# Mixer loads at other places: weight tiles, next values, p fetches, token sums and decay tables of a hybrid encoder layer

## The chip, the cores and the metric

The kernel runs on one core of one Trainium2 chip. The metric is the device time of one execution in microseconds (us); lower is better. The core has five engines with queues of their own: TensorE (PE, matrix products; its weight loads are shown as PEld), VectorE (DVE), ScalarE (ACT), GpSimd (POOL) and SyncE (SP), which here does nothing but issue DMA transfers. Each engine runs its instructions in order, and one that waits holds up all behind it.

## The reference

One post-norm layer of an encoder, in fp32, for x of 1024 tokens by 1024 features:

```
u    = x @ w_in                                   # split into rq, rk, rv, rg, aq, ak, av
yR   = swish(rg) * GroupNorm(retention fwd + bwd) # 8 heads of 64, chunks of 128, decays from ret_decay
yA   = windowed attention, +-128 tokens, 8 q heads on 2 kv heads, ALiBi, a sink logit per head
h    = LN1(alpha * x + concat(yR, yA) @ w_out)
f    = (silu(h @ w_gate) * (h @ w_up)) @ w_down + sigmoid(h @ w_ple_gate) * (p @ w_ple_proj)
out  = LN2(alpha * h + f)
```

`p` is 1024 tokens by 256. The decays of retention are log1p(-2^ret_decay), one per head and direction.

## The kernel before, in words

**Arithmetic.** An fp32 product is made of three matmuls of a faster type: each operand is cut into a high part (an ACT copy, recorded at L51) and a low part (a DVE subtraction, L107), by `split`, and `mm3` (L110 to L112) multiplies high by high, high by low and low by high. So every operand that PE uses passes through ACT and DVE first.

**Stages.** First the input projections of the parts that the mixers need at once, in units `punits` of a Strassen-like scheme (seven products for each pair of weight tiles, `Proj`); after unit 8 the loop calls `tables()`, which makes the decay tables: a power on POOL (L196), then a chain of small operations on DVE and two on ACT with table loads. Then the mixers, four pairs of heads i = 0 to 3, each with `Retention` (values rv, keys rk, queries rq, decay mask dt) and `Attention` (scores, sc, transposed by trn, multiplied by val). Then the output projection with LN1, the per-layer gate with p (`ple`), the feed-forward products, and LN2. After the mixers everything is one schedule written by hand; it includes the token sums of `ple`.

**The mixers.** The order of PE, POOL and SP is the order of the program text there. DVE and ACT are ordered by a scheduler, which by and large follows when operands come. Operations wrapped in `in_order` are chained on ACT and DVE to stay behind each other. A script (L836 to L848) lists the steps of a pair; each `F` in it takes the next few steps from a queue. This queue, built by `enqueue`, holds the rest of the projections as ten tiles of 16 steps: AQI[2], RKI[3], RQI[3], embedding(0), AQI[3], embedding(1) and four gates. A step of a projection is three matmuls of 128x512 (one `mm3`); the last of eight copies a bank to a tile `es` and stores it in DRAM (`ud`, L746; a gate multiplies it in place instead). While one tile's steps run, the next tile's raw weights are loaded and cut, attached to steps 0, 6, 9 and 12 of the tile before.

**Embedding.** `embedding(h)` multiplies p by one half of w_ple_proj. For each of 8 blocks t of tokens a fetch (L767) brings pT[t] to a tile `pr` (two buffers), `prep` cuts it to `p` (two buffers), two steps multiply, and the result goes through `es` to `ed` by SP (L797). At the first step of block t the kernel fetches t+2 and cuts t+1.

**Raw buffers.** Raw weights, q's raw tile (`load_pair`, L546) and rv's raw tile (`rv_load`, L537) share one ring `raw` of two buffers: a new load waits until the tile two before it is read. `load_pair(i+1)` loads rk, rq and q of the next pair (`more[0]` in the script), `rv_load(i+1)` its values (`more[1]`), `cq[g]` converts q, `nt[h]` transposes rv (PE, L523), to be copied by ACT.

**Token sums.** In `ple`, `to_T(t)` (L1009 on) builds for a block t of tokens the sums x1, x2 and x3 that the seven products need, and at once cuts x2 into TT[2] and stores a copy of h (`keep_h`). Side work is handed to `prod` in four slots per product.

Of the kernel before, what the change touches and what calls it, by code (L numbers as in the profile page):

```python
# [20 lines left out]
NT = S // P  # L21
# [19 lines left out]
def layer(tc, xT, xn, w_first, w_mt, w_out, w_pg, w_pe, pT, w_gu, w_dn,  # L41
# [21 lines left out]
    def in_order(f):  # L63

        def g(*args):
            behind_act[1] = True
            f(*args)
            behind_act[1] = False

        return g  # L70
# [107 lines left out]
    lt = cp.tile([P, 4, 24], F32, name="lt")  # L178
# [14 lines left out]
    def tables():  # L193
        t_, u_, d_, m_ = (lt[:, i, :] for i in range(4))
        pool.tensor_copy(masks, mraw)
        pool.tensor_tensor(t_, cst[:, C_TWO:C_TWO + 1].to_broadcast([P, 24]), rr, ALU.pow)  # L196
        dve.tensor_scalar(u_, t_, -1.0, 1.0, ALU.mult, ALU.add)
        act.activation(rr, u_, AF.Ln)
        dve.tensor_scalar(d_, u_, 1.0, None, ALU.subtract)
        dve.tensor_scalar(m_, d_, 0.0, None, ALU.is_equal)  # L200
        dve.tensor_tensor(d_, d_, m_, ALU.subtract)
        dve.tensor_tensor(rr, rr, m_, ALU.subtract)
        dve.reciprocal(m_, d_)
        dve.tensor_tensor(rr, rr, m_, ALU.mult)
        dve.scalar_tensor_tensor(lg, rr, -1.0, t_, ALU.mult, ALU.mult)
        act.activation(kd[:, 0, :], lg[:, 0:8], AF.Exp, scale=cst[:, C_KF:C_KF + 1])
        act.activation(kd[:, 1, :], lg[:, 8:16], AF.Exp, scale=cst[:, C_KB:C_KB + 1])
        dve.tensor_scalar(kd, kd, 0.125, None, ALU.mult)
        act.activation(cd, lg[:, 16:24], AF.Exp, scale=float(P))
        dve.tensor_scalar(skb, skb, -1.0, None, ALU.mult)  # L210
# [167 lines left out]
    with tc.manual_schedule(engines={ET.PE, ET.DVE, ET.Activation, ET.Pool, ET.SP}):  # L378
        zero = tt([P, HF], "s1", 2, mybir.dt.bfloat16)
        pool.memset(zero, 0.0)  # L380
        zb = bank("o")
        for _ in range(WARM):
            pe.matmul(zb, zero[:, :P], zero, start=True, stop=True)
        for (m, h), t in zip([(m, h) for m in range(4) for h in range(2)], [t for t in ("mm", "s", "t", "o") for _ in range(NB[t])]):
            st[m, h] = bank(t)
        for kt in range(KT):
            r = A[kt]
            if kt % 2 == 0:
                xp = big16()
            xt = xp[:, :, kt % 2, :]  # L390
            if kt == 0:
                w0 = rawt(2 * HF)
                sp.dma_start(w0[:, :HF], w_first[0][:, :HF])
                for h in range(2):
                    sp.dma_start(r[:, hs[h]], xT[kt][:, hs[h]])
                sp.dma_start(w0[:, HF:], w_first[0][:, HF:])

                def first_w(j):
                    wt_ = wp.tile([P, 2, HF], F32R, tag="w", bufs=4, name=nm("w"))
                    wr = w0[:, j * HF:(j + 1) * HF]  # L400
                    dve.tensor_copy(wt_[:, 0, :], wr)
                    dve.tensor_tensor(wt_[:, 1, :], wr, wt_[:, 0, :].bitcast(F32), ALU.subtract)
                    return wt_

                wf = [first_w(0)]
            else:
                if kt % 2 == 0:
                    wr = rawt(2 * HF)
                    sp.dma_start(wr, w_first[kt // 2])
                sp.dma_start(r, xT[kt])  # L410
                if kt % 2 == 0:
                    wf = []
                    for i in range(2):
                        t = wp.tile([P, 2, HF], F32R, tag="w", bufs=4, name=nm("w"))
                        split(wr[:, hs[i]], t[:, 0, :], t[:, 1, :])
                        wf.append(t)
            if kt == 1:
                wf.append(first_w(1))
            w = wf[kt % 2]
            for h in range(2):  # L420
                split(r[:, hs[h]], xt[:, 0, hs[h]], xt[:, 1, hs[h]])
            xs.append(xt)
            for m, h in ([(m, h) for m in range(4) for h in range(2)] if kt else [(m, h) for h in range(2) for m in range(4)]):
                mm3(st[m, h], w[:, 0, m * P:(m + 1) * P], w[:, 1, m * P:(m + 1) * P],
                    xt[:, 0, hs[h]], xt[:, 1, hs[h]], kt == 0, kt == KT - 1)
            if kt > 4:
                x_put(kt - 5)
            if kt >= 4:
                x_sums(kt - 4)
        for n in range(2):  # L430
            projs[n].load()
        consts_in()
        pahead(2)
        first = [atile() for _ in range(4)]
        for m in range(4):
            t = first[m]
            act.activation(t[:, hs[0]], st[m, 0], AF.Copy)
            dve.tensor_copy(t[:, hs[1]], st[m, 1])
        pahead(4)
        x_put(3)  # L440
        for k, (pr, p) in enumerate(punits):
            pr.mm(p)
            pr.post(p, k)
            if pr is projs[-1]:
                {6: lambda: keys(hs[0]), 5: lambda: keys(hs[1]), 7: lambda: queries(hs[0]),
                 2: lambda: queries(hs[1])}.get(p, lambda: None)()
            pahead(k + 1 + min(5, 4 + k))
            while late and late[0][0] <= k:
                late.pop(0)[1]()
            if k == 8:  # L450
                tables()
        for _, f in late:
            f()

# [47 lines left out]
    def enqueue(tiles):  # L502

        def both(f, g):
            f()
            g()

        for f in tiles[0][0]:
            f()
        for n, (_, steps) in enumerate(tiles):  # L510
            if n + 1 < len(tiles):
                for k, f in zip((0, 6, 9, 12), tiles[n + 1][0]):
                    steps[k] = lambda f=f if k == 0 else in_order(f), g=steps[k]: both(f, g)
            queue.extend(steps)


# [239 lines left out]
    def embedding(h):  # L756

        hold = {}

        wpe, ps = [], {}  # L760

        prs = {}

        def fetch(t):
            if t < NT:
                prs[t] = bt([P, 2 * P], "pr", 2)
                sp.dma_start(prs[t], pT[t])  # L767

        def prep(t):
            if t < NT:  # L770
                ps[t] = bt([P, 2, 2 * P], "p", 2, F32R)
                split(prs[t], ps[t][:, 0, :], ps[t][:, 1, :])

        raw = {}

        def load():
            raw["r"] = rawt(2 * HF)
            sp.dma_start(raw["r"], w_pe[h])
            fetch(0)
            fetch(1)  # L780

        def cut(q):
            wpe.append(atile((P, 2, HF), F32R))
            split(raw["r"][:, hs[q]], wpe[q][:, 0, :], wpe[q][:, 1, :])

        def step(t, q):
            if q == 0:
                fetch(t + 2)
                in_order(prep)(t + 1)
                hold["b"] = bank("mm")  # L790
            b, pt = hold["b"], ps[t]
            c = slice(q * P, (q + 1) * P)
            mm3(b, pt[:, 0, c], pt[:, 1, c], wpe[q][:, 0, :], wpe[q][:, 1, :], q == 0, q == 1)
            if q:
                e = bt([P, HF], "es", 2)
                act.activation(e, b, AF.Copy)
                sp.dma_start(ed[t][:, hs[h]], e)  # L797

        return [load, lambda: cut(0), lambda: cut(1), lambda: prep(0)], [lambda t=t, q=q: step(t, q) for t in range(NT) for q in range(2)]

    def run(steps, total):

# [10 lines left out]
    F = None  # L813
    with tc.manual_schedule(engines={ET.PE, ET.Pool, ET.SP}):
        enqueue([spill(AQI[2]), spill(RKI[3]), spill(RQI[3]), embedding(0), spill(AQI[3]), embedding(1)] + [gate(i) for i in range(4)])
        turn_rv = rv_load(0)
        for i in range(NPAIR):
# [4 lines left out]
            sco, trn, val = (lambda n: (a.scores, n)), (lambda n: (a.turn, n)), (lambda n: (a.values, n))  # L822
# [11 lines left out]
            else:  # L834
# [1 line left out]
            run(first_steps + [  # L836
                C(1), K(2), sco(1), F, C(2), K(3), F, trn(0), sco(2), ws[1], F, C(3), (r.scan,), val(0), F, trn(1), sco(3), F,
                val(1), Y(0, 0), ws[2], F, trn(2), sco(4), F, val(2), Y(0, 1), N(0), F, trn(3), sco(5), M(0), ws[3], F,
                val(3), Q(1), more[0], F, trn(4), sco(6), F, val(4), Y(1, 0), ws[4], F, trn(5), sco(7), more[1], cq[0], F,
                val(5), Y(1, 1), N(1), ws[5], F, trn(6), cq[1], F, nt[0], nt[1], val(6), M(1), F, trn(7), ws[6], F], 36)  # L840
            val_last = val(7)
        run([val_last, F, X(0), F, X(1), F, F], 16)

# [172 lines left out]
    def to_T(t):  # L1016
# [12 lines left out]
        dve.tensor_tensor(x2, b1, x1, ALU.subtract)  # L1029
        dve.scalar_tensor_tensor(HB[1, 1][:, 1, :, cols(t)], b1, -1.0, h.bitcast(F32), ALU.mult, ALU.subtract)  # L1030
        dve.tensor_tensor(x3, x3, b1, ALU.subtract)
        put(2, x2, t)
        keep_h(t, act)

    def t3(t):
# [57 lines left out]
    def ple(ahead):  # L1093
# [21 lines left out]
        def c00(k):  # L1115
            act.activation(g[k], b1[k], AF.Sigmoid)
            if k % 2:
# [4 lines left out]
        s1 = quad()  # L1122
        to_T(4)
        prod(1, b1, True, False, lambda k: act.activation(s1[k], b1[k], AF.Copy),
             [L(to_T, 5), L(t4s, 4), L(to_T, 6), L(t4s, 5)])
        g = quad()
        prod(2, b1, False, True, c00, [L(to_T, 7), [], L(t4s, 6), L(t4s, 7)])
        by = banks(TO)
        u2 = quad()
        prod(6, by, True, False, plus(u2, s1, by), [L(t3, 4), L(t3, 5), L(t3, 6), L(t3, 7)])  # L1130
# [540 lines left out]
```

## Time and profile before

| what | value |
|---|---|
| time, median of 3 runs | 1221.87 us (1220.24 to 1222.24) |
| time of the profiled execution | 1221.87 us |
| its span on the core | 1219.7 us |
| mean granted TensorE clock | 0.995 |
| DMA | 186.81 MB in 72848 packets, 153 GB/s over the span |
| loads `raw<-in_w_mt` | 14 of 512 KB, median 3.7 us to landing |

How to read it: the span runs from the first to the last instruction that the profiler recorded. A row of the timeline gives start, duration, engine, line, operation, the tile written and the tiles read, the shape, and in brackets how long the engine stood idle before it and who released it; equal rows in a line are merged (x4), and their duration is then that of all. "SPq" rows are DMA issues, and a landing is the time from the issue until the data are there. A row of waits gives the total, the number and the longest. Line numbers are those of the kernel before; in the changed kernel the same lines stand 3 to 6 further down inside the first stage and the mixers (L537 becomes L543, L546 becomes L552, L767 becomes L773).

### The profile page before, as it was taken

The numbers are of one execution on the slowest core, as the hardware profiler recorded it, in microseconds if no ns is written. First come the engines' busy times: TensorE is split into PE (matmuls) and PEld (weight loads), VectorE is DVE, ScalarE is ACT, GpSimd is POOL, SyncE is SP. The second block draws the span as 40 slices with busy tenths as digits, with TensorE's granted clock in tenths as the row PEclk, the third lists the DMA queues.
The fourth block names the chain that finished last, engine by engine and source line by source line (L and its number), as shares of the span: only waits on it lengthen the run. The fifth ranks groups of instructions, "written<-read, shape, count | busy, mean of one in ns | idle before, by whom it ended". The sixth has DMA issues, their size and how long they took to land.

```text
span 1219.7 us, 16421 instructions
## 1 busy us (share of the span) xinstructions
PE 1195.1 (98%) x5911; PEld 985.5 (81%) x5911; DVE 764.3 (63%) x1258; ACT 525.3 (43%) x968; POOL 448.5 (37%) x379
## 2 busy tenths in 40 slices
PE   9999999989799999999999999999999999999997
PEld 7878888768688788878888888888888888888886
DVE  6964666657565538776555555555545556875677
ACT  4532456666766512473433332333223334653441
POOL 1651213130201002332455655666556523024235
PEclk9999999999999999999999999999999999999999
DMA  6222255572310333445244344543544149999977
GB/s 224 92 87 104 83 177 153 159 224 95 114 35 22 123 114 106 143 176 181 104 164 122 103 155 165 181 128 97 155 165 146 70 144 288 386 277 211 273 172 207
DMA packets 72848, 186.81 MB, mean 153 GB/s; under 512 B 8384, under 2 KB 10560, under 8 KB 72768
## 3 DMA queue, kind: packets, MB, share of 16 engines
q1 hardware_dynamic: 57344, 148.03, 34.4%
q0 software_dynamic: 13696, 31.46, 13.6%
q10 hardware_dynamic: 1728, 6.29, 1.3%
q8 instruction: 46, 0.75, 0.2%
q14 instruction: 34, 0.28, 0.1%
HBM read 128.87 MB, written 51.64 MB: 148 GB/s over the span
## 4 chain that ended last, share of the span: by engine, by line
PE 90%; DVE 5%; DMA 2%; POOL 1%; issue 1%; ACT 1%; DVEq 0%; SPq 0%; POOLq 0%; ACTq 0%
PE bs L318 5%; PE bs L320 5%; PE bs L319 5%; PE bmm L320 5%; PE bmm L318 5%; PE bmm L319 5%; PE bt L318 5%; PE bt L320 5%; PE bt L319 5%; PE bo L320 5%; PE bo L318 5%; PE bo L319 5%; PE bmm L110 4%; PE bmm L112 4%; PE bmm L111 4%; PE bo L731 2%
## 5 line engine op out<-in xcount | busy, mean ns | idle before, releaser
L107 DVE TENSOR_TENSOR w<-H,w 128x512 fp32r<-128x512 f32 x44 | 43.6, 991 | 67.3 <-ACT w L51 67.3
L51 ACT ACTIVATE sc<-sc,st 128x385 f32<-128x385 f32 (+3 forms) x128 | 71.3, 582 | 27.0 <-DVE st L701 17.8
L1167 POOL TENSOR_TENSOR H<-ln 128x512 f32<-128x512 f32 x22 | 33.0, 1500 | 126.0 <-DMA ln<-in_w_gu 126.0
L107 DVE TENSOR_TENSOR w<-raw,w 128x512 fp32r<-128x512 f32 x56 | 44.3, 798 | 47.5 <-ACT w L51 47.3
L1199 POOL TENSOR_TENSOR ev<-ev 128x512 f32<-128x512 f32 x33 | 52.1, 1579 | 56.5 <-DMA h<-in_w_dn 24.1
L107 DVE TENSOR_TENSOR u<-H,u 128x512 fp32r<-128x512 f32 x47 | 45.4, 967 | 40.3 <-ACT u L51 40.2
L1203 POOL TENSOR_TENSOR ev<-ev,ev 128x512 f32<-128x512 f32 x44 | 67.3, 1539 | 2.6
L51 ACT ACTIVATE ev<-ev 128x512 f32<-128x512 f32 x33 | 20.9, 632 | 107.0 <-DVE ev L1214 107.0
L110 PE MATMUL bmm<-H,w 128*128 128x512 f32 x144 | 61.4, 426 | 0.2 <-ACT H L51 0.2
L696 POOL COPY sc<-skb 128x2 f32<-128x2 f32 x32 | 6.0, 191 | 140.6 <-PE bt L716 114.4
L112 PE MATMUL bmm<-H,w 128*128 128x512 f32 x144 | 57.2, 397 | 0.0
L111 PE MATMUL bmm<-H,w 128*128 128x512 f32 x144 | 57.1, 396 | 0.0
L51 ACT ACTIVATE w<-raw 128x512 fp32r<-128x512 f32 x72 | 43.6, 622 | 25.9 <-PE bo L112 6.2
L893 POOL TENSOR_TENSOR stt<-stt,cst 128x1 f32<-128x1 f32 x8 | 11.5, 1451 | 99.4 <-DVE stt L892 99.4
L51 ACT ACTIVATE u<-H 128x512 fp32r<-128x512 f32 x47 | 29.5, 628 | 38.9 <-POOL H L1169 8.8
L51 ACT ACTIVATE u<-raw 128x512 fp32r<-128x512 f32 x43 | 26.2, 629 | 29.6 <-PE bt L320 8.0
L51 ACT ACTIVATE w<-H 128x512 fp32r<-128x512 f32 x44 | 27.4, 622 | 23.3 <-PE bmm L320 6.6
L701 DVE CUSTOM_DVE_ANT_0 sc<-cst,bs,skb 128x384 f32<-128x384 f32 (+1 forms) x64 | 35.1, 575 | 2.5 <-PE bs L700 2.2
L1171 POOL TENSOR_TENSOR H<-ln,raw 128x512 f32<-128x512 f32 x22 | 34.3, 1562 | 0.0
L110 PEld LDWEIGHTS bmm<-H,w 128*128 128x128 f32 x144 | 27.6, 192 | 6.7 <-issue 1.5
L1169 POOL TENSOR_TENSOR H<-H,raw 128x512 f32<-128x512 f32 x22 | 32.1, 1461 | 1.7
L1314 POOL DMA_DIRECT2D h<-in_w_dn x24 | 21.3, 899 | 31.2 <-issue 16.6
(857 smaller groups left out, 3994.1 us busy)
## 6 DMA issues: line engine op xcount, KB each, us to landing
ad<-ev SPq DMA_DIRECT2D x33, 512.0 KB, 2.9
raw<-in_w_gu SPq DMA_DIRECT2D x22, 512.0 KB, 5.5
ln<-in_w_gu SPq DMA_DIRECT2D x22, 512.0 KB, 4.3
raw<-ad SPq DMA_DIRECT2D x40, 256.0 KB, 5.8
ln<-ad SPq DMA_DIRECT2D x37, 256.0 KB, 6.5
H<-in_w_dn SPq DMA_DIRECT2D x33, 256.0 KB, 8.0
raw<-in_w_mt SPq DMA_DIRECT2D x14, 512.0 KB, 3.7
A<-in_w_pg POOLq DMA_DIRECT2D x12, 512.0 KB, 5.5
```

The source lines that it names most:

```text
L51: ins = nc.scalar.activation(*args, **kw)
L107: dve.tensor_tensor(lo, raw, hi.bitcast(F32), ALU.subtract)
L110: pe.matmul(o, lh, rh, start=start, stop=False)
L111: pe.matmul(o, lh, rl, start=False, stop=False)
L112: pe.matmul(o, ll, rh, start=False, stop=stop)
L318: pe.matmul(o, lh, rh, start=start, stop=False, skip_group_check=True)
L319: pe.matmul(o, lh, rl, start=False, stop=False, skip_group_check=True)
L320: pe.matmul(o, ll, rh, start=False, stop=stop, skip_group_check=True)
L701: dve.tensor_tensor_reduce(sc[:, g, :nk], cst[:, tc0:tc0 + nk], b[:, :nk], -slope(i, g), skb[:, 2 * i + g:2 * i + g + 1], ALU.add, ALU.min ...
L1171: pool.tensor_tensor(s[2], a(1, 0), a(0, 0), ALU.subtract)
L1199: pool.tensor_tensor(c[:, 1, :], c[:, 0, :], c[:, 1, :], ALU.mult)
L1203: pool.tensor_tensor(self.ev[dst][:, 0, :], left, right, op)
```

## The change

Five edits, all of order; the number of instructions on each engine stays the same, and so does PE's order.

1. `tables()` keeps its two POOL operations after unit 8; its DVE and ACT operations become `tables2()`, after unit 16.
2. `enqueue` attaches the next tile's load and cuts to steps 8, 12 and 14 (for the third tile 2, 6 and 8); for an embedding, which now has five functions, to 6, 10, 12, 13 and 14.
3. `embedding` starts with begin(0) and begin(1), each of which cuts a block and fetches the one two further; at the end of block t, behind the store, it cuts t+2 and fetches t+4.
4. In the script, `more[1]` (rv's load) stands behind sco(6) instead of sco(7), and `cq[0]` behind Y(1, 1).
5. `to_T` loses its last two lines to a new `t2(t)`, which side slots of the first two products call later.

```diff
@@ tables
         pool.tensor_tensor(t_, cst[:, C_TWO:C_TWO + 1].to_broadcast([P, 24]), rr, ALU.pow)
+
+    def tables2():
+        t_, u_, d_, m_ = (lt[:, i, :] for i in range(4))
         dve.tensor_scalar(u_, t_, -1.0, 1.0, ALU.mult, ALU.add)
...
             if k == 8:
                 tables()
+            if k == 16:
+                tables2()
@@ enqueue
-                for k, f in zip((0, 6, 9, 12), tiles[n + 1][0]):
-                    steps[k] = lambda f=f if k == 0 else in_order(f), g=steps[k]: both(f, g)
+                fs = tiles[n + 1][0]
+                for j, (k, f) in enumerate(zip((6, 10, 12, 13, 14) if len(fs) > 3 else (2, 6, 8) if n == 1 else (8, 12, 14), fs)):
+                    steps[k] = lambda f=in_order(f) if j else f, g=steps[k]: both(f, g)
@@ embedding
             if q == 0:
-                fetch(t + 2)
-                in_order(prep)(t + 1)
                 hold["b"] = bank("mm")
...
                 sp.dma_start(ed[t][:, hs[h]], e)
+                in_order(prep)(t + 2)
+                fetch(t + 4)
+
+        def begin(t):
+            prep(t)
+            fetch(t + 2)
+
-        return [load, lambda: cut(0), lambda: cut(1), lambda: prep(0)], ...
+        return [load, lambda: cut(0), lambda: cut(1), lambda: begin(0), lambda: begin(1)], ...
@@ script of a pair
-                val(3), Q(1), more[0], F, trn(4), sco(6), F, val(4), Y(1, 0), ws[4], F, trn(5), sco(7), more[1], cq[0], F,
-                val(5), Y(1, 1), N(1), ws[5], F, trn(6), cq[1], F, nt[0], nt[1], val(6), M(1), F, trn(7), ws[6], F], 36)
+                val(3), Q(1), more[0], F, trn(4), sco(6), more[1], F, val(4), Y(1, 0), ws[4], F, trn(5), sco(7), F,
+                val(5), Y(1, 1), cq[0], N(1), ws[5], F, trn(6), cq[1], F, nt[0], nt[1], val(6), M(1), F, trn(7), ws[6], F], 36)
@@ to_T, ple
-        put(2, x2, t)
+
+    def t2(t):
+        put(2, X[t][1], t)
         keep_h(t, act)
...
-             [L(to_T, 5), L(t4s, 4), L(to_T, 6), L(t4s, 5)])
+             [L(to_T, 5) + L(t2, 4), L(t2, 5) + L(t4s, 4), L(to_T, 6), L(t2, 6) + L(t4s, 5)])
-        prod(2, b1, False, True, c00, [L(to_T, 7), [], L(t4s, 6), L(t4s, 7)])
+        prod(2, b1, False, True, c00, [L(to_T, 7), L(t2, 7), L(t4s, 6), L(t4s, 7)])
```

What this does to the order of an engine's rows is seen at three places. The first is SP in pair 2, from the end of embedding(1) to the load of rv for pair 3. `raw` is the ring of two, `rkq` holds rk and rq, `ed` and `es` are the embedding's stores; L141 loads the first gate's weight tile. Before:

```order
L797 DMA ed<-es_2919 128x512
L543 DMA rkq_2952<-ud 128x1024
L544 DMA rkq_2953<-ud 128x1024
L546 DMA raw_2956<-ud 128x1024
L797 DMA ed<-es_2963 128x512
L797 DMA ed<-es_3000 128x512
L141 DMA raw_3003<-in_w_mt 128x1024
L537 DMA raw_3058<-ud 128x1024
```

And after:

```order
L773 DMA pr_2810<-in_pT 128x256
L141 DMA raw_2840<-in_w_mt 128x1024
L801 DMA ed<-es_2849 128x512
L801 DMA ed<-es_2913 128x512
L549 DMA rkq_2949<-ud 128x1024
L550 DMA rkq_2950<-ud 128x1024
L552 DMA raw_2953<-ud 128x1024
L801 DMA ed<-es_2960 128x512
L543 DMA raw_2997<-ud 128x1024
L801 DMA ed<-es_3003 128x512
```

The weight tile has moved from behind q's raw tile to ahead of it. The load of rv therefore takes the buffer of the weight tile, no longer that of q's raw tile.

The second place is SP at the start of embedding(0); `pr` are the fetches of p, and L746 (L752) stores a projection's bank. Before:

```order
L778 DMA raw_1786<-in_w_pe 128x1024
L767 DMA pr_1788<-in_pT 128x256
L767 DMA pr_1790<-in_pT 128x256
L746 DMA ud<-es_1917 128x512
L746 DMA ud<-es_2040 128x512
L141 DMA raw_2070<-in_w_mt 128x1024
L767 DMA pr_2072<-in_pT 128x256
L797 DMA ed<-es_2084 128x512
L767 DMA pr_2104<-in_pT 128x256
```

And after:

```order
L784 DMA raw_1877<-in_w_pe 128x1024
L773 DMA pr_1879<-in_pT 128x256
L773 DMA pr_1881<-in_pT 128x256
L752 DMA ud<-es_1914 128x512
L773 DMA pr_2008<-in_pT 128x256
L773 DMA pr_2039<-in_pT 128x256
L752 DMA ud<-es_2047 128x512
L801 DMA ed<-es_2084 128x512
L773 DMA pr_2090<-in_pT 128x256
```

Blocks 2 and 3 are now fetched before the first step of the embedding, and the next tile's weight load (L141) is gone from among the fetches; it stands behind the last of them.

The third place is ACT at the first step of embedding(1), in pair 2. `sc` are attention scores, `p<-pr` the high parts of p, and the first `es` of each piece the copy of the last bank of the tile before the embedding, AQI[3]. Before:

```order
L51 ACTIVATE p_2598<-pr_2420 128x256
L51 ACTIVATE sc_2616,st_2579<-sc_2616,st_2579 128x385 x2
L51 ACTIVATE es_2652<-bmm_2549 128x512
L51 ACTIVATE sc_2616<-sc_2616,st_2579 128x384 x2
L51 ACTIVATE p_2659<-pr_2422 128x256
L51 ACTIVATE ptr_2674<-bt_2671 128x256
```

And after:

```order
L51 ACTIVATE sc_2613,st_2576<-sc_2613,st_2576 128x385 x2
L51 ACTIVATE es_2659<-bmm_2546 128x512
L51 ACTIVATE sc_2613<-sc_2613,st_2576 128x384 x2
L51 ACTIVATE p_2628<-pr_2484 128x256
L51 ACTIVATE p_2636<-pr_2486 128x256
L51 ACTIVATE ptr_2674<-bt_2671 128x256
```

The cut of block 0 has moved from ahead of that `es` to behind it and behind the two `sc` copies, next to the cut of block 1.

More of the change, by code (lines that the diff above doesn't have):

```diff
@@ L797, in step @@
                 sp.dma_start(ed[t][:, hs[h]], e)
-        return [load, lambda: cut(0), lambda: cut(1), lambda: prep(0)], [lambda t=t, q=q: step(t, q) for t in range(NT) for q in range(2)]
+                in_order(prep)(t + 2)
[3 more added lines that the diff above has]
+            fetch(t + 2)
+        return [load, lambda: cut(0), lambda: cut(1), lambda: begin(0), lambda: begin(1)], [lambda t=t, q=q: step(t, q) for t in range(NT) for q in range(2)]
     def run(steps, total):
```

## The prediction

> **What bounds the kernel now.** I read the page first, then TensorE's waits, then the timeline around each wait of the mixers, the decay tables and the token sums. Busy time and the chain of waits on the page, then who TensorE (PE) waited for (total us, times, longest):
>
> ```profile
> PE 1195.1 (98%) x5911; PEld 985.5 (81%) x5911; DVE 764.3 (63%) x1258; ACT 525.3 (43%) x968; POOL 448.5 (37%) x379
> ```
>
> ```profile
> engine line waited for: us in total, times, longest us
> PE bt L523 <- DMA raw<-ud: 6.0, 1, 6.0
> PE bmm L110 <- ACT p L51: 5.6, 6, 3.3
> PE bs L699 <- DVE pt L617: 0.8, 2, 0.6
> PE bt L318 <- DVE A L1113: 0.7, 1, 0.7
> PE bs L318 <- DVE A L297: 0.6, 1, 0.6
> PE bmm L112 <- DVE p L107: 0.6, 2, 0.4
> ```
>
> PE is the bound, and the change alters neither its instructions nor their order. So the change can only move PE's gaps. The rows name five it aims at: the transposition of rv (L523), the `p` splits (two rows), the token sums (L1113), the tables (L297). The row of L699 is one it may lengthen. The profiled execution took 1221.87 us, 2.17 more than its span of 1219.7; that is also the median of the three runs shown, so sums go against 1221.87. About 0.2% (2.4 us) is what a measurement of this kernel tells from no change.
>
> A wait costs PE a little more than its idle time. PE's timeline around the longest wait for `p` (start, duration):
>
> ```profile
> 254.01 0.40 PE L112 MATMUL bmm<-A,p 128*128 128x512 f32 x1
> 257.73 0.50 PE L110 MATMUL bmm<-A,p 128*128 128x512 f32 x1 [3.32 <-ACT p L51]
> 258.06 0.40 PE L111 MATMUL bmm<-A,p 128*128 128x512 f32 x1
> 258.30 0.39 PE L112 MATMUL bmm<-A,p 128*128 128x512 f32 x1
> 258.53 0.82 PE L716 MATMUL bt<-cst,sc 128*128 128x128 f32 x6
> ```
>
> Back to back these matmuls start 0.23 apart (258.30 to 258.53). Across the wait it is 3.72, so 3.49 is lost where 3.32 is listed: 0.17 more per wait.
>
> **Gains, part by part.** *The p waits.* ACT's timeline, and from the chain in order of time the two transfers of `pr` that end in long waits; then the landing of all 16:
>
> ```profile
> 257.26 0.42 ACT L51 ACTIVATE p<-pr 128x256 fp32r<-128x256 f32 x1 [3.50 <-DMA pr<-in_pT]
> ```
>
> ```profile
> 227.38 6.83 DMA pr<-in_pT
> 250.03 7.21 DMA pr<-in_pT
> ```
>
> ```profile
> DMA to landing us min/median/max: 1.9/3.3/7.2
> ```
>
> A fetch goes out two weight-tile steps ahead of its split, and what is late is the transfer that takes about 7 us, beside the 512 KB loads of the same queue; ACT, which runs in order, stands for it with an es copy behind. The change gives the fetch four steps and puts the loads behind the last fetches. With the median landing of 3.3 all eight waits go: 5.6 + 0.6 + 8 x 0.17 = 7.6. (With 7.2 some stay: a rival below.)
>
> *rv(3).* What SP's L537 waited for, its issue, the landing of its three transfers, and PE with its clock in stretches around it (length, PE busy, granted clock, DMA share):
>
> ```profile
> SPq L537 <- DVE q L354: 13.2, 1, 13.2
> ```
>
> ```profile
> 329.72 0.32 SPq L537 DMA_DIRECT2D raw<-ud x1
> ```
>
> ```profile
> DMA to landing us min/median/max: 3.1/3.5/3.7
> ```
>
> ```profile
> 226.20:263.10 36.90, 31.12 (x230) 1.00 0.73 226
> 266.59:269.86 3.27, 3.27 (x27) 1.00 0.33 94
> 332.95:338.51 5.56, 5.56 (x26) 0.56 0.42 106
> ```
>
> ```profile
> 326.80:331.00 4.20, 0.19 (x1) 1.00 0.06 17
> 331.00:338.00 7.00, 5.05 (x24) 0.51 0.47 145
> ```
>
> The load wanted the raw buffer that the q conversions of pair 3 held. In the changed order the first gate's weight tile is loaded ahead of load_pair(3), so of the two buffers rv(3) takes that tile's, free at its second cut, which stands some eight weight-tile steps before the transposition. A step takes about 1.9 (31.1 busy for 16, in the row of 226.20 above), so the load has some 15 us for its 3.5. The wait goes, 6.0 + 0.17 = 6.1. So does the slow clock behind it: 4.2 us into the idle stretch the granted clock falls to 0.51, and the matmuls from L523 to the next L716 took 5.56 against 3.27 a pair earlier: 2.3.
> The Trainium skill (TensorE: Matmul & The Clock Gate, What's actually happening) says the same of the cause, half the pulses after an idle window of about 3.4 us and full clock after as long a busy one; by it the debt would be 3.4 us at half speed, so 1.7 us in place of 2.3, and the forecast 0.6 higher. Here the clock came back 6.8 us after it fell, 5.05 of them busy.
>
> *Tables and token sums.* POOL's pow, for which DVE's and ACT's table operations stood in order, with PE's A (L297) behind them, and DVE's half of the u splits, ahead of L1113:
>
> ```profile
> 73.95 4.62 POOL L196 TENSOR_TENSOR lt<-cst,rr 128x24 f32<-128x24 f32 x1
> ```
>
> ```profile
> 536.40 2.50 DVE L948 TENSOR_TENSOR u<-raw,u 128x512 fp32r<-128x512 f32 x4 [3.38 <-ACT u L51]
> ```
>
> The pow now has eight units of products to end in, and the short operations behind it start at once. The wait of 0.6 + 0.17 goes, though DVE still has them to do: 0.2 is left as a loss (0 to 0.8, the old wait). In the sums, ACT's split of x2 waited for DVE ahead of the copies and u splits that DVE then waited 3.38 for. With t2 put later ACT comes to them sooner than PE's 0.7 was late, and 0.7 + 0.17 goes; t2's own split and store then have two products to hide in, and cost 0.7 again if those were full. Together 1.6. All gains: 7.6 + 6.1 + 2.3 + 1.6 = 17.6.
>
> **Losses, part by part.** *Entry of the two embeddings.* begin(0) hangs on step 14, but ACT keeps its own order: the first p split now stands behind the es copy of the step before the embedding's first, and behind two sc copies. ACT and PE there:
>
> ```profile
> 224.35 1.12 ACT L51 ACTIVATE sc<-sc,st 128x384 f32<-128x384 f32 x2 [0.23 <-DVE st L706]
> 224.59 0.39 PE L112 MATMUL bmm<-H,w 128*128 128x512 f32 x1
> 226.18 0.39 PE L110 MATMUL bmm<-A,p 128*128 128x512 f32 x1
> ```
>
> ```profile
> 285.22 0.39 PE L110 MATMUL bmm<-A,p 128*128 128x512 f32 x1
> 285.42 0.60 ACT L51 ACTIVATE es<-bmm 128x512 f32<-128x512 f32 x1 [0.52 <-PE bmm L112]
> 285.91 1.11 ACT L51 ACTIVATE sc<-sc,st 128x384 f32<-128x384 f32 x2
> 286.92 0.40 ACT L51 ACTIVATE p<-pr 128x256 fp32r<-128x256 f32 x1
> ```
>
> At the second, es and sc at 285.42 and 285.91 are followed by p at 286.92, and the changed order has the *first* p there: ready at 287.32, where PE wants it at 285.22, 2.1 late, and 0.2 of refill: 2.3. Nothing covers it, as PE goes from the last step of one tile to the first of the next without mixer work between. At the first embedding the step before ends at 224.59 + 0.39 = 224.98; from there es 0.6, sc 1.1 and p 0.4 end at 227.1, where PE wants p at 226.18 (mixer work lies between): 0.9, and 0.2 of refill: 1.1. Bounds: 0, if ACT is through with sc before es is due, and 2.3 at each. Both stay under the 3.3 of idle at 254 that did not slow the clock.
>
> *ACT between pairs.* Both conversions of q now stand ahead of the copies of rv. ACT's row at i = 2, where table loads stand among them:
>
> ```profile
> 326.61 0.63 ACT L51 ACTIVATE sq<-ym 128x512 f32<-128x512 f32 x1 [0.49 <-DVE ym L654]
> 327.27 1.05 ACT L51 ACTIVATE q<-raw 64x1024 fp32r<-64x1024 f32 x1
> 329.00 1.28 ACT L51 ACT_TABLE_LOAD   x1
> 330.29 0.60 ACT L51 ACTIVATE es<-bmm 128x512 f32<-128x512 f32 x1
> 334.08 0.60 ACT L51 ACTIVATE rv<-bt 128x512 f32<-128x512 f32 x1 [0.60 <-PE bt L523]
> ```
>
> Chained from 326.61, without the weight split that left: 327.27 + 1.05, table load 1.28, es 0.6, rv twice 0.6, less 0.1 of overlap each: 331.4. PE, with rv there, would want the bank for trn(7) 3.27 behind L523 at 327.0, at 330.3: 1.1 late; 0.3 more for the second table load ahead of the decay mask, and 0.2 of refill: 1.6. Bounds 0, and 2.9 with a second load in full. The Trainium skill (ScalarE: Activation LUTs, What ACT_TABLE_LOAD costs) speaks against the change here: it gives a load 1.28 us and a drain of about 1.38 besides. The rows show es 1.29 after the load's start and no such drain; by the page the loss would be 1.4 more and the forecast 1211.8. Between pairs 1 and 2, with no table load, the same costs 0.4.
>
> *Small ones.* In pair 2 a p split and a w split stand ahead of pt on DVE: the waits of the row of L699 get 0.4 longer (0 to 0.8, the row over again). POOL does its part of a token split (L948) ahead of a LayerNorm pow instead of behind it; DVE waits for that pow with time to spare, so I cost it at nothing, and at most at the 0.7 of the row of L1113. Tables: 0.2, from above.
>
> Losses: 2.3 + 1.1 + 1.6 + 0.4 + 0.4 + 0.2 = 6.0. 1221.87 - 17.6 + 6.0 = **1210.3 us**.
>
> **The rivals.**
>
> *Clean removal.* ACT's order costs PE nothing, as it is busy for 43% of the span and may run ahead: 1221.87 - 17.6 = 1204.3. Against it speaks the chain from 285.42 to 286.92, which starts with PE's own last step. 0.15.
>
> *p is still late.* Fetches may still take the 7.2 of the longest. A buffer's round in the changed order is its landing, then es and sc ahead of the split, the split on ACT (0.42) and DVE (about as long), then the SP issue: an estimate of landing + 3.1 (es 0.6, sc 1.1, the splits, and SP's 0.3 twice). PE's four steps take 7.8 (31.12 for 16). With 7.2 to land, 10.3 - 7.8 = 2.5 are lost. Two such landings, as in the chain before: 1215.3. For it: the same bytes move as before. Against it: the median of 3.3, and that the 512 KB loads now stand behind. 0.16.
>
> *rv(2) is late instead.* Its load now waits for the second cut of a weight tile. From 258.53 (trn(5)) I estimate its issue at +3.45 (sco(7), its two reductions and the w split on DVE, an ed store on SP) and its landing at +6.95, where L523 wants it at 266.59, +8.06: slack 1.1. The row for q's load on the same queue, L546:
>
> ```profile
> DMA to landing us min/median/max: 6.1/9.3/9.6
> ```
>
> With 9.3 to land it comes 4.7 late, over the 4.2 after which the clock fell: 4.7 + 2.3 more, 1217.3. Against it: L537's own three landed in 3.1 to 3.7. 0.08.
>
> *The ring of raw buffers turns the same way after all,* and rv(3) waits as before: 6.1 + 2.3 back, 1218.7, at the edge of 0.2%. Against it: the order of SP's rows. 0.04.
>
> *Slower: every fetch lands like the worst.* ed stores and fetches share SP in one order with two pr and two p buffers, so a late split holds the next fetch and the store behind it, and the loop runs at its own 10.3 per four steps, where before only the two long transfers cost much. Three rounds in each of two embeddings lose 2.5 each, 15: 1225.3 with the clock kept. It costs from a landing of 4.7 (7.8 - 3.1) on, and makes the kernel slower than before once the median reaches 6.6 (11.6 over six rounds, 1.9 each). The median of 3.3 is far under that, the highest of 7.2 over. 0.05.
>
> **How the numbers follow.** The forecast has 0.52, the others 0.15, 0.16, 0.08, 0.04 and 0.05. The range goes from 1204.3 (clean) to 1217.3 (rv(2) late) and leaves out the last two rivals, 0.09, and what the others' own sizes may be off by. Faster by over 0.2% (under 1219.4): forecast, clean, late p and half of rv(2)'s, with 1217.3 near the line: 0.87. Within: that other half and the ring, 0.08. Slower: 0.05.
>
> **What would show it.** Right: no row of PE for L523's raw; the row for `ACT p` at two waits of about 1 and 2, at the embeddings' first steps; a granted clock near 1.00 through the end of pair 2; short waits at trn(7). Wrong: waits for p inside an embedding with pr landing above 4.7 (late p or the slow loop), or L523 waiting at pair 1's end (rv(2)). Under 1206 would mean that ACT's order cost nothing; over 1219.4, that a new wait took the gain.

## The result, and the profile after

The changed kernel takes 1214.82 us (median of 4 runs, 1212.94 to 1215.94), the kernel before 1221.22 (4 runs, 1220.24 to 1222.24): 6.4 us less, a ratio of 0.9946 with a 95% interval of 0.9929 to 0.9963. The forecast was 1210.3 with a range of 1204.3 to 1217.3. The gain is there, but of the 11.6 us that were forecast about 5 are missing.

The profiled execution took 1212.94 us, with a span of 1211.1, 8.6 under that of before. About 2 of these 8.6 belong to no edit. Both kernels do the same first 10 us, and in one stretch of it PE got through 12 matmuls before and 20 after; columns are length, PE busy (matmuls), granted clock, DMA share, GB/s. Before:

```profile
5.40:10.00 4.60, 4.60 (x12) 1.00 1.02 358
```

After:

```profile
5.40:10.00 4.60, 4.60 (x20) 1.00 0.99 377
```

The kernel before starts its matmuls of 128x512 0.43 apart up to 10.3 us and 0.23 apart from then on; the changed kernel is at 0.23 from 5.7 on. Runs of one and the same kernel differ by this much, and the medians average over it. PE has the same matmuls in the same order in all kernels here, so in what follows two profiles are laid against each other matmul by matmul, start to start, and differences before 55 us are left out. What remains of the change is 6.6, which agrees with the medians' 6.4.

Whom PE waited for in the changed kernel (total us, times, longest). Its lines stand 3 to 6 further down: L529 was L523, L722 was L716, L705 was L699.

```profile
engine line waited for: us in total, times, longest us
PE bmm L110 <- ACT p L51: 2.7, 2, 2.1
PE bmm L110 <- ACT es L51: 2.0, 1, 2.0
PE bt L529 <- DMA raw<-ud: 1.7, 1, 1.7
PE bs L705 <- DVE pt L623: 1.3, 3, 0.6
PE bmm L112 <- DVE p L107: 0.9, 2, 0.5
PE bt L722 <- ACT rv L51: 0.9, 2, 0.5
```

Against the rows of before: the wait of 6.0 for rv, the six for the high part of p, the tables and the token sums are gone. Two waits for p stand at the embeddings' first steps, two for rv's copies at trn(7), as forecast. Two rows are new and hurt: `es` with 2.0, and another load of rv with 1.7. Where pair 2 ends, PE now runs through, L529 straight behind the gate's matmuls, and waits only for rv's copy at L722:

```profile
325.75 0.40 PE L112 MATMUL bmm<-H,w 128*128 128x512 f32 x1
325.99 1.04 PE L529 MATMUL bt<-cst,raw 128*128 128x128 f32 x8
...
329.93 0.93 PE L722 MATMUL bt<-cst,sc 128*128 128x128 f32 x4 [0.50 <-ACT rv L51]
```

The two new rows hang together. ACT at the time of the new wait, and PE behind it:

```profile
250.80 0.49 ACT L51 ACTIVATE ptr<-bt 128x384 f32<-128x384 f32 x1 [1.65 <-PE bt L722]
256.00 0.60 ACT L51 ACTIVATE es<-bmm 128x512 f32<-128x512 f32 x1 [4.70 <-DMA ed<-es]
256.49 0.62 ACT L51 ACTIVATE w<-raw 128x512 fp32r<-128x512 f32 x1
```

```profile
256.65 0.50 PE L110 MATMUL bmm<-H,w 128*128 128x512 f32 x1 [1.99 <-ACT es L51]
...
263.66 0.52 PE L529 MATMUL bt<-cst,raw 128*128 128x128 f32 x3 [1.70 <-DMA raw<-ud]
```

The chain that ended last, in order of time, over the same place:

```profile
243.95 0.20 SPq L550
...
244.20 0.50 SPq L552
...
244.79 11.18 DMA ed<-es
...
256.00 0.03 ACT es L51
...
256.49 0.63 ACT w L51
...
257.15 0.70 DVE w L107
...
257.87 0.32 SPq L543
```

Read it from the top. SP issues the loads of rk, rq (L550) and q (L552) for pair 2, right behind the weight load of the next tile; next in its queue is the embedding's store ed<-es, and that takes 11.18 us to land. The es tile is therefore taken, one of two. ACT stands 4.70 for it, and holds a PSUM bank that PE needs (1.99). Behind the es copy stands the second cut of the weight tile, and rv's load (L543) waits for that cut's buffer and then takes 5.66 to land, so L529 is late as well (1.70). The landings of the 16 stores to ed in both kernels (us, min, median, max), before and then after:

```profile
DMA to landing us min/median/max: 2.0/2.2/7.4
```

```profile
DMA to landing us min/median/max: 2.0/2.8/11.2
```

The fetches of p land no sooner than before by their median (3.5 against 3.3), but inside the embeddings they are no longer waited for (after):

```profile
DMA to landing us min/median/max: 2.0/3.5/6.4
```

Between the two new waits PE ran slowly. Stretches of the changed kernel:

```profile
254.50:256.60 2.10, 0.16 (x2) 1.00 0.03 12
...
257.50:260.90 3.40, 3.40 (x13) 0.52 1.00 230
```

And of before, where PE had stood longer at this place:

```profile
254.00:257.70 3.70, 0.41 (x2) 1.00 0.94 360
257.70:262.00 4.30, 4.27 (x35) 1.00 0.68 213
```

After 2.1 us of rest the clock fell to half for 3.4 us; after 3.3 of rest before it had not.

### The profile page after: what moved, and what is told of

Read it like the earlier page. It is cut to its first block, busy times and chain, and to the rows that moved or that the text cites. A ratio compares the mean times of both kernels' runs of the same rounds, so it can differ in the third digit from the quotient of the medians.

```text
span 1211.1 us, 16411 instructions
## 1 busy us (share of the span) xinstructions
PE 1191.4 (98%) x5911; PEld 983.4 (81%) x5911; DVE 764.6 (63%) x1258; ACT 523.6 (43%) x968; POOL 449.0 (37%) x379
## 4 chain that ended last, share of the span: by engine, by line
PE 93%; DVE 3%; DMA 2%; ACT 1%; issue 1%; POOL 1%; SPq 0%; DVEq 0%
PE bs L323 6%; PE bs L321 6%; PE bs L322 6%; PE bmm L322 6%; PE bmm L323 6%; PE bmm L321 6%; PE bt L322 5%; PE bt L323 5%; PE bt L321 5%; PE bo L321 5%; PE bo L322 5%; PE bo L323 5%; PE bmm L110 4%; PE bmm L111 4%; PE bmm L112 4%; PE bo L737 2%
```

## The experiments

The theory after the result has two losses. At the entries of the embeddings ACT has p behind es; at 244 to 256 the stores stand behind a crowd of 512 KB loads. Each median below goes with the runs of before that shared its chip.

**The weight load out of the crowd** (e1_load_early).

```diff
-... (2, 6, 8) if n == 1 else (8, 12, 14)
+... (2, 6, 8) if n == 1 else (2, 12, 14) if n == 3 else (8, 12, 14)
```

> The changed kernel, with the weight load of tile AQI[3] at step 2 of embedding(0) instead of step 8, so that it no longer stands right ahead of the loads of rk, rq and q of pair 2. Theory (the stores of es stand on SP behind a burst of four 512 KB loads, the es buffer stays taken, and with it ACT, a bank, the cut and the rv load): PE's wait for es (2.0), the slow clock after it (about 1.2) and the wait for rv's raw tile (1.7) go, 5 us in all, so about 1209.6 where the changed kernel takes 1214.8. Rival (three loads are as bad as four, since the store lands behind the last of them anyway): no change, 1214.8. Second rival (fetches of p now stand behind that load): waits for p of 1 to 3 us in embedding(0), 1213 to 1216.

Measured: 1215.97 against 1222.35, ratio 0.9945 (0.9933 to 0.9958): no change against the changed kernel, as the first rival said. The wait for es is still there on ACT, a little longer, and now the copy `ptr` stands behind it, so PE waits sooner, at val(5):

```profile
256.49 0.60 ACT L51 ACTIVATE es<-bmm 128x512 f32<-128x512 f32 x1 [5.26 <-DMA ed<-es]
...
257.50 0.48 ACT L51 ACTIVATE ptr<-bt 128x384 f32<-128x384 f32 x1
```

```profile
PE bo L737 <- ACT ptr L51: 3.7, 1, 3.7
```

The es and rv rows of PE are gone, and one of 3.7 stands for both. Three loads are as bad as four: the longest store still takes 10.1 us. My expectation that a burst one load shorter would be cheap was wrong.

**The first cuts of p earlier** (e2_entry).

```diff
-(6, 10, 12, 13, 14) if len(fs) > 3
+(2, 6, 8, 10, 11) if len(fs) > 3
```

> The changed kernel, with the five functions of an embedding at steps 2, 6, 8, 10 and 11 instead of 6, 10, 12, 13 and 14, so that the first two cuts of p stand on ACT ahead of the es copy of the tile before. Theory (p waits at the two entries because of ACT's order): the waits of 0.8 and 2.2 go, about 1211.8 for 1214.8. Rival (ACT is simply full there and the wait moves to the next thing, sc or es): same as the changed kernel within 1 us.

Measured: 1211.55 against 1222.35, ratio 0.9911 (0.9896 to 0.9926), 4 us under the changed kernel by the ratios. Both waits for p have left PE's rows. Laid against the changed kernel, the two first steps of the embeddings come 0.80 and 2.22 sooner, and all else stays within 0.7. The price that the prediction gave these two, 1.1 and 2.3, was right in mechanism and size.

**Both** (e3_both).

> Both edits of the two runs before. If the two losses are independent they add: about 8 us under the changed kernel, 1206.8. If one hides behind the other, 1209 to 1211.

Measured: 1213.52 against 1222.35, 0.9933 (0.992 to 0.9945). They do not add, since the first repairs nothing: PE's wait at val(5) for ptr is 4.4 there, and the gain at the entries is half eaten.

**Stores on ACT's queue** (e4_edact).

```diff
-                sp.dma_start(ed[t][:, hs[h]], e)
+                act.dma_start(ed[t][:, hs[h]], e)
```

> The changed kernel, with the embedding's stores to ed issued from ACT's queue instead of SP's. If the late store is due to its place in SP's queue behind the loads, it lands in about 3 us, PE's wait for es goes with the slow clock and the rv wait, 5 us, against 16 issues of 0.33 us on ACT, which has room except at the entries and between pairs: 1210 to 1212. If it is due to the DMA engines being full whoever issues, the store still lands in 8 to 11 us and the wait stays: 1214 to 1216.

Measured: 1210.45 against 1222.35, 0.9901 (0.9887 to 0.9914). ACT at the same place, and the landings of the 16 stores:

```profile
251.98 0.60 ACT L51 ACTIVATE es<-bmm 128x512 f32<-128x512 f32 x1 [0.93 <-DMA ed<-es]
```

```profile
DMA to landing us min/median/max: 2.0/3.0/8.6
```

ACT stands 0.93 instead of 4.70, and PE's rows for es and for rv's load are gone. The store that the copy waits for now takes 7.65 us to land. It is in a queue without loads, and it goes out between the issues of rk's and rq's loads (at 244.25) instead of behind all four; which of the two counts is not separated here. At 8.6 at worst a store beside the loads is still slow. Both readings held a part.

**The script's edit alone** (e5_more_only), in the kernel before.

```diff
-trn(4), sco(6), F, ..., trn(5), sco(7), more[1], cq[0], F, val(5), Y(1, 1), N(1)
+trn(4), sco(6), more[1], F, ..., trn(5), sco(7), F, val(5), Y(1, 1), cq[0], N(1)
```

> The kernel before, with only the script's edit: rv's load two shares earlier and the first conversion of q behind Y(1, 1). Theory A (as the prediction has it: the weight tile's place in the ring frees rv(3), so the edit of enqueue is needed): the wait for rv(3) stays, about 1221, or 1.4 later through ACT's order between pairs. Theory B (what counts is that rv's load comes ahead of the second gate's weight load, by whichever edit): the wait of 6.1 and the slow clock of 2 go, trn(7) costs up to 1.4, so about 1214.5; the second gate's weight load then waits for q's buffer, with time to spare.

Measured: 1216.63 against 1222.75, 0.996 (0.9939 to 0.998). No row for L523 is left in PE's waits; laid against before, 6.1 are gone there, the slow clock too, with 0.7 and 0.9 given back at trn(7) and its neighbour. Theory B holds. The prediction's account of the ring was wrong: the weight load that stood between q's and rv's loads before was the second gate's, not the first's. What frees rv(3) is that its load comes ahead of that one; either edit does it.

**The edit of enqueue alone** (e6_enq_only).

> The kernel before, with only the edit of enqueue (loads at step 8, cuts at 12 and 14; for an embedding 6, 10, 12 and 14). Both theories expect the rv(3) wait and the slow clock gone, 8 us. p is fetched as before, so its waits stay, less the first one of 1.2 beside the weight load that left, but with four loads in a row behind step 56 instead of three: a wait of 3.5 to 6 there. About 1213.

Measured: 1219.35 against 1222.75, 0.9972 (0.9959 to 0.9985). rv(3) no longer waits, and p waits longer:

```profile
PE bmm L110 <- ACT p L51: 8.0, 6, 4.8
```

The longest is 4.8, where ACT's p stands behind an es that waits 3.39 for its store. It is 6 us worse than expected: the profile shows 0.8 and 2.2 lost at the entries, which the expectation had left out, 1.4 more at the longest wait, and 2.3 of slow clock behind it.

**The edit of embedding alone** (e7_emb_only), its begin functions at steps 12 and 13.

> The kernel before, with only the edit of embedding (its begin functions at steps 12 and 13, other tiles as before). The waits for p inside the embeddings go (7.7); the entries cost 3.0; the store of es behind three loads costs 0 to 2; rv(3) waits as before. About 1217.5; if the wait for es took the place of all of the wait for p, 1220.

Measured: 1219.21 against 1222.75, 0.997 (0.9958 to 0.9982), between the two numbers. The waits for p fall by 7.7, with rv(3) as before, and at 254 the place of p's wait is taken by `ptr`:

```profile
PE bt L524 <- DMA raw<-ud: 6.2, 1, 6.2
PE bo L732 <- ACT ptr L51: 2.3, 1, 2.3
```

This is the es wait again, with the weight load at step 0 as before. So it comes with the loads of the next pair, not with the moved weight load. The entries cost nothing here (0.0 at both first steps); the cuts of p at steps 12 and 13 start early enough.

**Tables and token sums alone** (e8_tab_t2).

> The kernel before, with only tables2 and t2. Theory: the two waits go, 0.8 and 0.9 to 1.1, so about 1219.4, and nothing else moves. Rival (the mixers take their start elsewhere when the tables come later): a later wait of up to 1 in pair 0, 1221.

Measured: 1220.79 against 1222.75, 0.9992 (0.9978 to 1.0006): by itself not to be told from no change. The profiles show both gains, 0.88 between 70 and 90 us and 1.08 between 530 and 545, at the places that the edit names. The waits that it leaves alone scatter by up to 0.7.
The profile shows one thing more. PE's wait at 254 is there as before, and this time the clock fell behind it:

```profile
254.90:258.30 3.40, 3.33 (x12) 0.50 0.62 198
```

2.6 us are lost there that the edit has nothing to do with.

**Both repairs that work** (f1_entry_edact): the first cuts at 2, 6, 8, 10, 11 and the stores on ACT's queue.

> The changed kernel with the embeddings' functions at steps 2, 6, 8, 10 and 11 and the stores to ed on ACT's queue: the two repairs that helped alone. If the losses at the entries (3.0) and behind the loads (4.4) are separate, they add to 7.4 under the changed kernel: about 1207.5. If ACT's extra issues of 0.33 us meet the earlier cuts of p, 1209 to 1210.

Measured: 1206.8 against 1223.22, ratio 0.987 (0.9857 to 0.9883). They add. What is left of PE's waits in the mixers is small:

```profile
PE bs L705 <- DVE pt L623: 1.8, 4, 0.6
...
PE bo L737 <- DVE ptr L727: 0.9, 2, 0.7
PE bmm L112 <- DVE p L107: 0.8, 1, 0.8
...
PE bt L722 <- ACT rv L51: 0.5, 1, 0.5
```

This is the best version of the study, 16.4 us under before, where the changed kernel was 6.4 under the runs of before on its own chip.

**The loads on POOL's queue instead** (f2_entry_poolloads), with the first cuts early.

```diff
-        sp.dma_start(rk, ud[RKI[i]])
+        pool.dma_start(rk, ud[RKI[i]])
```

and the same for rq and q.

> The changed kernel with the embeddings' functions at steps 2, 6, 8, 10 and 11 and the loads of rk, rq and q of the next pair on POOL's queue instead of SP's; the stores stay on SP. If the late store is a matter of standing behind the loads in one queue, this is as good as moving the stores: about 1208. If it is the load on the DMA engines, 1211 to 1212 as with the entries alone. If POOL's copies of sk into sc now wait behind loads that wait for their buffers, PE waits for scores: over 1213.

Measured: 1214.54 against 1223.22, 0.9931 (0.9919 to 0.9943): the third number, but not for the reason given with it. The loads of rk, rq and q have left SP's queue, and yet the slowest store there lands as late as before:

```profile
DMA to landing us min/median/max: 2.0/2.4/11.2
```

It still stands behind the next tile's weight load, and that is now late itself, so that ACT waits for it first:

```profile
243.28 10.55 DMA raw<-in_w_mt
```

```profile
253.85 0.63 ACT L51 ACTIVATE w<-raw 128x512 fp32r<-128x512 f32 x1 [4.47 <-DMA raw<-in_w_mt]
```

So it is not a matter of the three loads in SP's queue alone. In these 12 us more is asked for than can land at once: the DMA share in the changed kernel is 0.93 from 243 to 246 us, 1.04 to 249 and 0.91 to 252. The queues change which transfer is the late one, and it costs when ACT, in order, stands for it.

Two transfers of 512 KB on POOL's queue, for the sums of the gate weights, lie in the same stretch (A<-in_w_pg, issued at 240.91, and ws<-A at 246.45); no run here moved them, so what they add is open.

**q's second conversion behind rv** (f3_f1_cq), in the kernel with both repairs.

```diff
-trn(6), cq[1], F, nt[0], nt[1], val(6), M(1), F, trn(7)
+trn(6), F, nt[0], nt[1], val(6), cq[1], M(1), F, trn(7)
```

> As the kernel with both repairs, and the second conversion of q behind the transpositions of rv instead of ahead of them. If trn(7) waits because ACT converts q ahead of copying rv, the two waits of 0.5 each and what hangs on them (0.6 to 0.8 a pair) go: 1.5 under it, about 1206. If the table load and es ahead of the copies are what counts, only pair 1 gains: 1207. If q is then late for the first scores of the next pair: a new wait for q of up to 1, 1207.5 to 1208.5.

Measured: 1214.71 against 1223.22, 0.9924 (0.9903 to 0.9944), 8 us worse, and with more scatter than any other (1208.2 to 1219.1). The profiled run is the slowest of the six. trn(7) between pairs 2 and 3 does come 0.67 sooner, but at the end of pair 0 q's second low half now stands on DVE ahead of a copy that PE needs. It takes 2.42 there, against 1.22 in the kernel with both repairs, and PE waits 3.0:

```profile
205.36 2.42 DVE L357 SCALAR_TENSOR_TENSOR q<-raw,q 64x1024 fp32r<-64x1024 f32 x1
207.71 0.41 DVE L727 COPY ptr<-bt 128x256 f32<-128x256 f32 x1
```

I had looked at q's readers and not at what stands behind its conversion. Behind the wait the granted clock is 0.50 from 208.2 to 214 us. Together that is 5.7, about half of what this run lost. The other half lies in embedding(0): ACT stands 5.01 for a projection's store ud<-es that took 9.9 to land, PE waits 2.2 for ptr, and the clock is 0.51 from 242 to 248.5. That this second loss comes from the edit is not shown; the fastest run, at 1208.2, cannot have had both.

**rk's load earlier** (f4_rk_early), in the kernel with both repairs: `load_pair` cut in two, rk's load behind N(0).

> As the kernel with both repairs (early embedding functions, stores to ed on ACT's queue, 1206.8), and the load of rk of the next pair two shares ahead of those of rq and q, into the third rkq buffer, which is free. If the crowd of 512 KB loads within some 12 us is what makes its neighbours late, the ed stores and the weight load land 1 to 2 us earlier and what is left of waits beside them (about 1) goes: 1206. If nothing behind the loads waits any more in that kernel, no change: 1206.8. If the early load hits the fetches of p, waits of 1 to 3 for p: 1208 to 1210.

Measured: 1207.63 against 1223.37, 0.9876 (0.9855 to 0.9898): no change. The longest landing of a weight tile falls from 7.1 to 6.8 and that of p from 8.3 to 7.5, but that of the stores stays (8.4 and 8.3), and a wait of 1.6 for ptr appears behind an es that stands 1.90 for its store:

```profile
251.97 0.60 ACT L51 ACTIVATE es<-bmm 128x512 f32<-128x512 f32 x1 [1.90 <-DMA ed<-es]
```

The store that counts is as late as before, so nothing is won.

## Why the prediction was right, and where it was not

*The gains were right, term by term.* Laid matmul by matmul: tables 0.88 for 0.8 less 0.2, the sums 1.08 for 0.9, rv(3) 6.1 for 6.1, the starts that waited for p 7.9 together for 7.6. At the end of pair 2 the sum with the slow clock and the new wait at trn(7) is 7.2, against 8.4 less 1.6.

*The losses that were foreseen were right too.* The entries cost 0.81 and 2.22 for 1.1 and 2.3, shown by the run that took them away. trn(7) costs 0.9 and 1.0, for 0.4 and 1.6: together 1.9 for 2.0. (Of the 1.6, 0.2 was a slip: the chain that ends at 331.4 does not take off the overlaps that it names, and with them it ends at 331.2.) The wait for rv's copy at the second, behind the table load, is 0.50. The Trainium skill (ScalarE: Activation LUTs, What ACT_TABLE_LOAD costs) would have it 1.38 longer by a drain; the trace does not show one.

*The step that failed* is the sentence that the change "puts the loads behind the last fetches", taken as pure gain, with all of the 3.49 at 254 as removed. Behind the loads in the same queue stands the next store to ed, and that I never priced. The wait of 3.49 went, and 2.18 for es came in its place, with 1.6 of slow clock behind it and 1.86 for rv(2): 5.7 in all, more than had been won there. The low half of p, on DVE, costs 0.6 twice besides (at 242 and 310), for which the sum had only the 0.4 of pt. Of the 11.6 forecast 5.0 are missing, and 6.6 are measured; so the other terms together came out 1.9 better (5.7 + 1.2 - 1.9 = 5.0), in small parts.

*A rival named part of it for another reason.* "rv(2) is late instead" gave its load's own landing of 9.3 as the cause, and 4.7 + 2.3 as the price. It was late by 1.86, and its slack of 1.1 was indeed short. Two things made it so: it was issued only at 257.87, because the cut that it waits for was held up by the es copy, and it took 5.66 to land, where that rival's own estimate of the slack had 3.5 and its price 9.3. Had it landed in 3.5, it would have been there at 261.4, before PE wanted it at 262.0. "p is still late" named the right place (12 us of crowded transfers) and the wrong victim.

*One step was right by its number only.* rv(3) was freed, but not for the reason given: the text on the order takes raw_3003 of before for the first gate's weight tile, and the prediction builds on its having moved ahead of q's load. It is the second's (the first's was loaded ahead of q's in the kernel before as well), and the run with the script's edit alone shows that no move of a weight load is needed.

*The slow clock.* The prediction tied it to 4.2 us of rest. The runs show that it is not a matter of that length alone: after the same wait of 3.3 at 254 it stayed in one run and fell in another (e8_tab_t2), in the changed kernel it fell after 2.1, and after the wait of 2.3 for ptr in e7_emb_only it stayed.

## What to carry to other kernels

When a wait for a transfer is to be removed by asking earlier, look at what else goes through the same queue in the same 10 us: if the DMA engines are as full as they were here, some transfer is late, and the question is whose. Let it be one that no in-order engine stands for, and look up what is queued behind each thing that can. A store is a wait too, as soon as its buffer is wanted again.

## What the runs showed of the hardware

Half clock is partly luck in time: 3.3 us of rest gave full clock in one run and half clock, for 3.4 us, in another, 2.1 us of rest gave half clock in a third, and 2.3 gave full clock in a fourth (e7_emb_only: PE busy 0.18 of the 2.50 us up to 256.40, then 1.00). The first 10 us differ between runs by about 2 us. The clock row reads 1.00 there in both kernels, so that the clock is the cause is inferred from the pace alone: 0.43 from start to start is also what these matmuls show at a granted clock of 0.52 (257.53 to 257.95 in the changed kernel). The Trainium skill (TensorE: Matmul & The Clock Gate, What's actually happening) has a window of about 3.4 us that runs freely and does not start with the kernel; the lengths of 3.4 us at half clock and the scatter at 254 agree with it. That 2.1 us of rest within such a window are enough is not what its one idle window says, and is measured here once.

A transfer of 256 KB that lands in 2.0 us at best took 11.2 behind four loads of 512 KB in one queue, and 8.6 at worst beside them in another queue; each time transfers of 512 KB on POOL's queue ran beside them.
